# The last three steps of an expert decoding: two interleaved, the weight remainders given to another engine, 36 matmuls put behind them

## The chip, the cores and the metric

The kernel runs on one core of one Trainium2 chip. The metric is the device time of one execution in microseconds (us), the median of several runs. A core has a matrix engine (TensorE, in the profile PE, its weight loads PEld), a vector engine (VectorE, DVE), an activation engine (ScalarE, ACT), a general engine (GpSimd, POOL) and an engine that here only issues transfers (SyncE, SP). Each works through its own queue of instructions in the order in which they were written. They wait for each other through semaphores.

## The reference

One encoder layer on 512 tokens of 1024 channels in float32: a projection, a gated branch and an attention branch, an output projection, and then the part that matters here, a retrieval over 128 x 128 = 16384 small experts:

```
q = (xb @ w_query).reshape(tokens, 8 heads, 2, 128)
s = einsum('thpc,pkc->thpk', q, sub_keys)             # 2 x 128 scores per token and head
s1, i1 = top_k(s[:, :, 0], 16); s2, i2 = top_k(s[:, :, 1], 16)
cand = s1[..., :, None] + s2[..., None, :]             # 256 sums
sc, ci = top_k(cand, 16)
e = i1[ci // 16] * 128 + i2[ci % 16]                   # 16 experts per token and head
g = softmax(sc)
act = gelu(einsum('td,thkd->thk', xb, expert_u[e]))
out = einsum('thk,thkd->td', g * act, expert_v[e])
```

## The kernel before, in words

The first three blocks of 128 tokens (384 tokens) are computed densely: for each of 128 slices of 128 experts TensorE multiplies all 384 tokens with a slice of `expert_u` ("a product of U"). A fourth block goes by gathers much later.

A product of U keeps float32 precision by splitting both operands in two parts. Slice i is loaded into `uraw` by SyncE's queue (`load`, two buffers). ScalarE rounds it into `uhi` (`part`, line 171, two buffers). Another engine subtracts, `ulo = uraw - uhi` (`part_lo`, line 182, two buffers). Then TensorE does 24 matmuls (line 202) in three passes of eight: `uhi` with the high part of the tokens, `uhi` with their low part, and `ulo` with the high part. The sum lands in a `pu` buffer (two of them), which ScalarE empties with a gelu into `act` (`flush`, line 789). A load needs the `uraw` buffer of the slice two before, which is free when that slice's `ulo` is made.

While `prog["pool"]` is true, GpSimd makes `ulo` in two halves, issued from `part` and inside `product`. Once it is false, the caller `los()` has VectorE make it whole.

`ahead(n, limit)` issues the next n matmuls of U. It is the filler: it is called between steps of the routing, whose long work is on VectorE. AHEAD = 31 products are to be done by the end of the routing. The routing runs so:

- For each of 16 query slices `scores` gives `sc`, and VectorE finds the 16 best in three lists (`top16`, lines 624 to 632). `candidates` (line 648) and `pick_head` (`top16` on `cand`) follow for each head. `decode` turns the choice into expert numbers for groups of 3, 3 and 2 heads. It is a generator with five pieces: comparisons on VectorE (lines 670 to 688), nothing, copies by ScalarE into one-hot tiles `oh` (lines 697 and 698, first from `rw`, then from `cl`), products on VectorE (lines 702 to 707), sums on VectorE into `route` (lines 711 to 717). `oh` has three buffers and one decoding uses two.
- `softmax` makes the gates (a subtraction on VectorE, an exponential on ScalarE, a normalisation on VectorE).
- At the end of the 16 slices, the second decoding (heads 3 to 5) is half done, the choice for head 7 and the third decoding (heads 6 and 7) are still to come. Before the change the second one is finished, then head 7 is chosen, then the third one runs, with `ahead(24)` or `ahead(36)` between the pieces.
- `turn` transposes the three routing tables on TensorE (`idxT` and `gT`). Then a loop over 48 groups of 8 tokens follows ("the one-hot loop"): VectorE makes `ohb` (a comparison) and `oha` (its product with the gates `gw`), TensorE multiplies them in 16 small matmuls, ScalarE copies the result to `wst`, and `left // 48` or so matmuls of U fill each group. In it VectorE makes `ulo`.

After the loop the U products go on, now together with the products of `expert_v` (line 1090).

Of the kernel before, what the change touches and what calls it, by code (L numbers as in the profile page):

```python
# [11 lines left out]
BF16 = mybir.dt.bfloat16  # L12
# [3 lines left out]
ALU = mybir.AluOpType  # L16
# [11 lines left out]
NK = 128  # L28
# [10 lines left out]
AHEAD = 31  # L39
# [7 lines left out]
def peer_block(ctx: ExitStack, tc: tile.TileContext, A, out):  # L47
    nc = tc.nc
    V, S, G, T, Q = nc.vector, nc.scalar, nc.gpsimd, nc.tensor, nc.sync
# [89 lines left out]
    iota_b = keep.tile([128, NK], BF16, name="iota_b")  # L139
# [18 lines left out]
    prog = {"u": 0, "gen": None, "gelu": None, "pool": True}  # L158
    halves = {}

    def load(i):
        if i < NQ + NK:
            raws[i] = upool.tile([128, KT, 128], F32, name="uraw")
            Q.dma_start(raws[i], A["w_q"][i] if i < NQ else A["uT"][i - NQ])
# [12 lines left out]
    def part_lo(i, eng=G):  # L177

        if i in halves:
            hi, lo = parts[i]  # L180
            k = slice(4 * halves[i], 4 * halves[i] + 4 if eng is G else KT)
            eng.tensor_tensor(lo[:, k, :], raws[i][:, k, :], hi[:, k, :].bitcast(F32), op=ALU.subtract)  # L182
            halves[i] += k.stop // 4 - halves[i]
            if halves[i] == 2:
                del raws[i], halves[i]

    def los():
        for i in list(halves):
            part_lo(i, V)
# [68 lines left out]
    def drain(gen, n=10 ** 6):  # L258
        for _ in range(n):
            if next(gen, True):  # L260
                return
# [22 lines left out]
    def heads_T(which, rot):  # L284


        for p in range(4):
            ps = pr.tile([128, 512], F32, name=("tr", "po")[p % 2])
            for b in range(NB):
                T.transpose(ps[:, b * 128:(b + 1) * 128], rot[:, b, p * 128:(p + 1) * 128], ident)  # L290
            two = tk.tile([128, 2, 512], F32R, name="qk2", tag="qk", bufs=8)
            klo = h2T[1][:, 2 * p:2 * p + 2, :]
            for j in range(2):
                own, other = (slice(64 * i, 64 * i + 64) for i in (j, 1 - j))
                hi = two[own, j, :]
                S.copy(hi, ps[own])
                lo = two[other, j, :] if which == "q" else klo[own, j, :]
                V.tensor_tensor(lo, ps[own], hi.bitcast(F32), op=ALU.subtract)
                if which == "k":
                    G.tensor_copy(two[other, j, :], hi.bitcast(F32))  # L300
                    G.tensor_copy(klo[other, j, :], lo.bitcast(F32))
            qk[which].append((two, klo if which == "k" else None))
            yield
# [39 lines left out]
    turning = heads_T("q", rot)  # L343
# [25 lines left out]
    turning = heads_T("k", rot)  # L369
# [25 lines left out]
    for b in range(NB):  # L395
        t = va[:, b, :]
# [168 lines left out]
    for b in range(NB):  # L565
        t = hs[b] = tk.tile([128, 1024], F32, name="xs", bufs=4)
# [45 lines left out]
    rt = rt_ctx.enter_context(tc.tile_pool(name="rt", bufs=1))  # L612
# [107 lines left out]
    def softmax(pool, top, g):  # L720

        PK = list(top.shape)
        V.tensor_tensor(g, top, top[:, :, :, 0:1].to_broadcast(PK), op=ALU.subtract)
        yield
        S.activation(g, g, AF.Exp)
        yield
        sm = pool.tile([128, 2, PK[1], PK[2]], F32, name="gsum")
        V.tensor_reduce(sm[:, 0], g, axis=AX.X, op=ALU.add)
        V.reciprocal(sm[:, 1], sm[:, 0])
        V.tensor_tensor(g, g, sm[:, 1, :, :, None].to_broadcast(PK), op=ALU.mult)  # L730
        yield
# [34 lines left out]
    steps = []  # L766

    def step():
        while steps:
            if next(steps[0], True) is None:  # L770
                return
            steps.pop(0)

    def pick_head(h):
        cand = cands.pop(h)
        top16([(top[:, h, b, :], ci[:, h, b, :], cand[:, b, :]) for b in range(DB)])
        h0 = 0
        for n in HG:
            if h == h0 + n - 1:
                steps.append(decode(rt, iota_v, dense[1][:, h0:h0 + n], ci[:, h0:h0 + n], [r[:, h0:h0 + n] for r in by_head]))  # L780
            h0 += n
# [3 lines left out]
    def flush():  # L785
        if prog["gelu"] is not None:
            e, o = prog["gelu"]
            acts[e] = ring.tile([128, DT], F32, name="act")
            S.activation(acts[e], o[:, :DT], AF.Gelu_apprx_tanh)  # L789
            prog["gelu"] = None  # L790

    def ahead(n, limit):

        while n > 0:
            if prog["gen"] is None:
                if prog["u"] >= min(limit, NK):
                    return
                i = prog["u"] + NQ
                load(i + 2)
                part(i + 1)  # L800
                prog["gen"] = product(i, DT)
            o = next(prog["gen"])
            n -= 1
            if o is not None:
                flush()
                prog["gelu"] = (prog["u"], o)
                prog["gen"] = None
                prog["u"] += 1

    for c in range(NQ + 1):  # L810
# [4 lines left out]
        if c >= 1:  # L815
# [4 lines left out]
                cands[(c - 1) // 2] = candidates(rt, dense, (c - 1) // 2)  # L820
            elif c > 1:
                pick_head((c - 1) // 2 - 1)
    while steps:
        ahead(24, AHEAD)
        flush()
        step()
    pick_head(H - 1)
    gating = softmax(rt, top, by_head[2])
    next(gating)
    step()  # L830
    for _ in range(4):
        ahead(36, AHEAD)
        flush()
        next(gating, None)
        step()
    assert not steps or next(steps[0], True)
    tsc = {}

    def turn(b):

        rows = []
        for nm, t, dt, scale in (("i2T", route[1], BF16, 1.0), ("i1T", route[0], BF16, 1.0),
                                 ("gT", route[2], F32, GSCALE)):
            ps = pr.tile([128, 512], F32, name="po" if nm == "i2T" else "tr")
            T.transpose(ps[:, :128], t[:, b].rearrange("p h k -> p (h k)"), ident)
            if nm == "i2T":

                idx = rt.tile([128, 16, 2, 8, 2], BF16, name="idxT", bufs=2)
            r = idx[:, :, len(rows), :, :] if dt is BF16 else rt.tile([128, 16, 8, 2], F32, name=nm)
            S.activation(r, ps[:, :128].rearrange("p (g t) -> p g t", t=8)[:, :, :, None].to_broadcast([128, 16, 8, 2]),  # L850
                         AF.Copy, scale=scale)
            rows.append(r)
        gT = rows[2]
        yield

        gw = rt.tile([128, 16, 8, 2, 2], F16, name="gw", bufs=2)
        V.tensor_copy(gw[:, :, :, 0], gT)
        V.tensor_tensor(gw[:, :, :, 1], gT, gw[:, :, :, 0], op=ALU.subtract)

        gs = rt.tile([128, 16, 2], F32, name="gs", bufs=2)  # L860
        V.tensor_copy(gs[:, :, 0], gw[:, :, 7, 0, 0])
        V.tensor_tensor(gs[:, :, 1], gT[:, :, 7, 0], gs[:, :, 0], op=ALU.subtract)
        tsc[b] = (idx, gw, gs)
        yield

    drain(turn(0))
    prog["pool"] = False


    half = [128, 16, NK // 2, 2]  # L870

    def hots(t8):


        b, g = divmod(t8, 16)
        idx, gw, gs = tsc[b]
        pairs = lambda t: t.rearrange("p s t two -> p (s t) two")[:, :, None, :].to_broadcast(half)
        c = rt.tile([128, 16, NK], BF16, name="ohb", bufs=3)
        a = rt.tile([128, 16, NK], F16, name="oha", tag="oh", bufs=3)
        V.tensor_tensor(c.rearrange("p s (k two) -> p s k two", two=2),  # L880
                        iota_b.rearrange("p (k two) -> p k two", two=2)[:, None, :, :].to_broadcast(half),
                        pairs(idx[:, g]), op=ALU.is_equal)
        wide = [128, 7, 2, NK // 2, 2]
        V.tensor_tensor(a[:, 0:14].rearrange("p (t s) (k two) -> p t s k two", s=2, two=2),  # L884
                        c[:, 8:15, None].rearrange("p t o (k two) -> p t o k two", two=2).to_broadcast(wide),
                        gw[:, g, 0:7, :, None, :].to_broadcast(wide), op=ALU.mult)
        rest.append((a, c, gs, g))
        return a, c
# [9 lines left out]
    N8 = DT // 8  # L898
    per = WTOK // 8
    wst = None  # L900
    hot = [hots(0), hots(1)]
    gated()
    ahead(24, AHEAD)
    los()
# [16 lines left out]
    for t8 in range(N8):  # L921
        a, c = hot.pop(0)
# [3 lines left out]
        for q in range(2):  # L926
            pw = pr.tile([128, 4, NK], F32, name="acc", bufs=4)
            for j in range(4):
                for s in range(2):
                    t = 4 * q + j  # L930
# [7 lines left out]
        if t8 % 16 == 8 and t8 // 16 + 1 < DB:  # L938
            turning = turn(t8 // 16 + 1)
# [220 lines left out]
    for e in range(NK):  # L1160
# [18 lines left out]
        n = min(int(quota), 128 - dotted)  # L1179
# [18 lines left out]
        if e == NK - 8:  # L1198
            assert issued == 128
            fg, *rest = [upool.tile([128, 1024], F32, name="fin", tag=t) for t in ("uraw", "uhi", "ulo") for _ in range(2)]  # L1200
            last = ex.tile([128, 2, 1024], F32, name="fin", tag="uv", bufs=UVB)
# [19 lines left out]
    for b in (0, 1):  # L1221
        vproduct(NK - 1, b)
        for n in range(2):
            c = slice(n * 512, (n + 1) * 512)
# [74 lines left out]
```

## Time and profile before

| what | value |
|---|---|
| median of 3 runs | 1474.46 us (1473.89 to 1474.46) |
| profiled execution | 1474.9 us, of which the span from first to last instruction is 1473.1 us |
| TensorE busy | 98% of the span |
| VectorE busy | 78% of the span |
| ScalarE, GpSimd busy | 45%, 19% |
| mean granted TensorE clock | 0.997 of full speed |

The span and the time differ by 1.8 us that lie around the instructions. A busy share is an average over stages; in the stage of the change VectorE is busy nearly all the time too.

### The profile page before, as it was taken

To read this page: it belongs to the slowest core of one execution; us is meant where nothing else is said; L and a number is where in the kernel's file an instruction comes from. 1 tells how busy PE (TensorE), PEld (TensorE's weight loads), DVE (VectorE), ACT (ScalarE), POOL (GpSimd) and SP (SyncE) were. 2 spreads that over 40 slices of the span, in tenths; PEclk is the share of its full clock that TensorE was granted. 3 is DMA by queue.
4 is the path that set the end of the run, shared out by engine and by line. 5 is a ranking of instruction groups with operands and counts; after the bars stand their busy time and mean duration, and the time that the engine had idled before them with its cause. 6 is when DMAs were issued, how large, how long until landed. Compare 5 with 4: busy or idle time off the path is not lost.

```text
span 1473.1 us, 21706 instructions
## 1 busy us (share of the span) xinstructions
PE 1449.5 (98%) x7945; PEld 1291.3 (88%) x7945; DVE 1152.5 (78%) x2434; ACT 658.0 (45%) x1186; POOL 278.3 (19%) x222
## 2 busy tenths in 40 slices
PE   8999999999999999999999999999999999999997
PEld 6878988888999999999999999999999999988785
DVE  5745554999899949779888878888888888877865
ACT  4456743344578754433333333333333333333334
POOL 0140002445400000013131222222222222221000
PEclk9999999999999999999999999999999999999999
DMA  6331032232367776579999998999999999988764
GB/s 232 113 103 36 23 130 104 74 97 92 115 248 267 275 276 215 165 264 368 351 332 336 330 341 318 335 332 345 331 336 339 327 326 338 321 299 302 232 215 152
DMA packets 129067, 358.54 MB, mean 243 GB/s; under 512 B 9152, under 2 KB 59840, under 8 KB 112576
## 3 DMA queue, kind: packets, MB, share of 16 engines
q1 hardware_dynamic: 103328, 197.49, 40.5%
q0 software_dynamic: 18432, 134.23, 23.8%
q10 hardware_dynamic: 7200, 25.44, 4.3%
q8 instruction: 62, 1.02, 0.3%
q14 instruction: 45, 0.37, 0.1%
HBM read 327.10 MB, written 30.02 MB: 242 GB/s over the span
## 4 chain that ended last, share of the span: by engine, by line
PE 82%; DVE 11%; ACT 3%; issue 2%; DMA 1%; POOL 1%; ACTq 0%; SPq 0%; POOLq 0%; DVEq 0%
PE acc L1090 34%; PE pu L202 32%; PE acc L253 8%; DVE ohb L880 3%; DVE ulo L182 2%; DVE oha L884 2%; PE pu L253 1%; PE tr L440 1%; PE acc L453 1%; PE po L453 1%; DMA vraw<-in_uv_dram 1%; POOL ulo L182 1%; ACT uhi L171 1%; DMA uraw<-in_uT_dram 1%; PE pu L419 0%
## 5 line engine op out<-in xcount | busy, mean ns | idle before, releaser
L202 PE MATMUL pu<-h2T,uhi 128*128 128x384 f32 (+2 forms) x2336 | 450.2, 342 | 1.8 <-ACT uhi L171 0.9
L202 PEld LDWEIGHTS pu<-h2T,uhi 128*128 128x128 f32 x2336 | 408.8, 188 | 18.1 <-ACT uhi L171 1.2
L1025 POOL DMA_INDIRECT uv<-in_uv_dram,ei x128 | 172.1, 1344 | 664.4 <-DVE xlast L1040 295.9
L82 DVE TENSOR_TENSOR vlo<-vraw,vhi 128x1024 fp32r<-128x1024 f32 x126 | 154.4, 1226 | 152.6 <-ACT vhi L81 152.5
L81 ACT CAST vhi<-vraw 128x1024 fp32r<-128x1024 f32 x126 | 132.5, 1052 | 304.7 <-issue 193.3
L202 PE MATMUL pu<-h2T,ulo 128*128 128x384 f32 (+2 forms) x1168 | 235.1, 340 | 2.6 <-POOL ulo L182 2.6
L1090 PE MATMUL acc<-vhi,wahi 128*128 128x512 f32 x756 | 234.9, 391 | 0.0
L1090 PE MATMUL acc<-vlo,wahi 128*128 128x512 f32 x756 | 234.6, 391 | 0.0
L1090 PE MATMUL acc<-vhi,walo 128*128 128x512 f32 x756 | 234.2, 391 | 0.0
L202 PEld LDWEIGHTS pu<-h2T,ulo 128*128 128x128 f32 x1168 | 204.2, 188 | 7.8 <-POOL ulo L182 3.4
L1090 PEld LDWEIGHTS acc<-vlo,wahi 128*128 128x128 f32 x756 | 141.5, 188 | 32.4 <-DVE vlo L82 1.4
L1090 PEld LDWEIGHTS acc<-vhi,walo 128*128 128x128 f32 x756 | 141.5, 188 | 31.0 <-DVE walo L82 0.7
L171 ACT CAST uhi<-uraw 128x1024 fp32r<-128x1024 f32 x144 | 150.4, 1045 | 40.7 <-DMA uraw<-in_uT_dram 34.6
L1040 DVE SCALAR_TENSOR_TENSOR xlast<-uv,dot,xlast 128x1024 f32<-128x1024 f32 x128 | 164.4, 1285 | 4.5
L789 ACT ACTIVATE act<-pu 128x384 f32<-128x384 f32 x128 | 62.9, 491 | 232.9 <-PE pu L202 232.8
L1090 PEld LDWEIGHTS acc<-vhi,wahi 128*128 128x128 f32 x756 | 140.6, 188 | 23.5
L1031 DVE SCALAR_TENSOR_TENSOR uv<-uv,h 128x1024 f32<-128x1024 f32 x128 | 153.8, 1219 | 7.9 <-DMA uv<-in_uv_dram,ei 7.6
L182 DVE TENSOR_TENSOR ulo<-uraw,uhi 128x1024 fp32r<-128x1024 f32 x116 | 141.5, 1219 | 18.4 <-ACT uhi L171 12.1
L182 POOL TENSOR_TENSOR ulo<-uraw,uhi 128x512 fp32r<-128x512 f32 x56 | 79.3, 1439 | 198.3 <-PE acc L253 104.8
L1068 DVE TENSOR_TENSOR wa<-act,wt 128x384 f32<-128x384 f32 x128 | 70.5, 551 | 0.8 <-DMA wt<-wd 0.8
L82 DVE TENSOR_TENSOR walo<-wa,wahi 128x384 fp32r<-128x384 f32 x126 | 69.6, 552 | 0.6 <-ACT wahi L81 0.6
L81 ACT CAST wahi<-wa 128x384 fp32r<-128x384 f32 x126 | 64.1, 509 | 9.1 <-DVE wa L1068 9.1
(274 smaller groups left out, 1511.5 us busy)
## 6 DMA issues: line engine op xcount, KB each, us to landing
uraw<-in_uT_dram SPq DMA_DIRECT2D x128, 512.0 KB, 5.9
vraw<-in_uv_dram SPq DMA_DIRECT2D x128, 512.0 KB, 5.6
wd<-wst ACTq DMA_DIRECT2D x48, 512.0 KB, 3.6
wt<-wd SPq DMA_DIRECT2D x32, 768.0 KB, 11.1
wraw<-in_w_in_dram SPq DMA_DIRECT2D x19, 512.0 KB, 3.7
uraw<-in_w_q_dram SPq DMA_DIRECT2D x16, 512.0 KB, 3.9
xT<-in_xT_dram SPq DMA_DIRECT2D x8, 256.0 KB, 3.6
xt<-in_x_dram SPq DMA_DIRECT2D x1, 2048.0 KB, 11.1
```

What stands on the lines that cost most here:

```text
L81: S.copy(hi, src)
L82: sub.tensor_tensor(lo, src, hi.bitcast(F32), op=ALU.subtract)
L171: S.copy(hi, raws[i])
L182: eng.tensor_tensor(lo[:, k, :], raws[i][:, k, :], hi[:, k, :].bitcast(F32), op=ALU.subtract)
L202: T.matmul(o, l[:, k, :], r[:, k, t0:n], start=(p == 0 and k == 0), stop=(p == 2 and k == KT - 1))
L253: T.matmul(out[b], l[:, b * 128:(b + 1) * 128], r[:, kk, :], start=(k == 0 and i == 0), stop=(k == KT - 1 and i == 2))
L789: S.activation(acts[e], o[:, :DT], AF.Gelu_apprx_tanh)
L1025: G.indirect_dma_start(out=uvs[r].rearrange("p s d -> p (s d)"), out_offset=None, in_=A["uv"], in_offset=bass.IndirectOffsetOnAxis(ap=ei[: ...
L1031: V.scalar_tensor_tensor(uv[:, 0, :], uv[:, 0, :], 1.0, h2, op0=ALU.mult, op1=ALU.mult, accum_out=d[:, 0:1])
L1040: V.scalar_tensor_tensor(xlast, uv[:, 1, :], d[:, 1:2], xlast, op0=ALU.mult, op1=ALU.add)
L1068: eng.tensor_tensor(wa.rearrange("p (c t) -> p c t", c=NWC), acts.pop(e).rearrange("p (c t) -> p c t", c=NWC), wts[e // WG][:, :, e % WG, ...
L1090: T.matmul(acc[b][n], l[:, c], r[:, n * 512:(n + 1) * 512], start=(e == 0 and i == 0), stop=(e == NK - 1 and i == 2))
```

## The change

GpSimd's part in `ulo` ends when the 16 slices are done, not after the first `turn`. From there `chunk(n)` issues n matmuls of U, then VectorE's `ulo` for each slice that has been split, then the gelu. The two last decodings are interleaved: head 7 is chosen ahead of the products of the second decoding, and the comparisons of the third come before the sums of the second. Until the transposes 216 matmuls of U are issued where there were 252 (with the 12 that both have before); the 36 that are missing go to the one-hot loop, which has 504 matmuls of U to place where it had 468. The first comparison `ohb` is written ahead of the four small operations that split the gates.

```diff
-    while steps:
-        ahead(24, AHEAD)
+
+    prog["pool"] = False
+
+    def chunk(n):
+        ahead(n, AHEAD)
+        los()
         flush()
-        step()
+
+    chunk(24)
+    step()
     pick_head(H - 1)
+    last = steps.pop()
     gating = softmax(rt, top, by_head[2])
     next(gating)
+    chunk(24)
     step()
-    for _ in range(4):
-        ahead(36, AHEAD)
-        flush()
-        next(gating, None)
-        step()
-    assert not steps or next(steps[0], True)
+    next(last)
+    chunk(24)
+    step()
+    step()
+    next(gating)
+    next(last)
+    next(last)
+    chunk(36)
+    next(gating)
+    next(last)
+    chunk(36)
+    next(last)
+    chunk(36)
+    chunk(24)
+    assert not steps and next(last, True) and next(gating, True)
...
-        yield
+        yield idx
...
-    drain(turn(0))
-    prog["pool"] = False
...
+    def match(ix):
+        c = rt.tile([128, 16, NK], BF16, name="ohb", bufs=3)
+        V.tensor_tensor(... op=ALU.is_equal)
+        return c
...
-    hot = [hots(0), hots(1)]
+    turning = turn(0)
+    first = match(next(turning)[:, 0])
+    drain(turning, 1)
+    hot = [hots(0, first), hots(1)]
```

VectorE's queue after the last list of the 16 slices, before the change: from the last candidates straight to the products of the second decoding (`oh`), then its sums, and no `ulo` in sight.

```order
L632 MAX_INDEX i_2180<-s_2179,sc 128x8 x3
L648 TENSOR_TENSOR cand<-s_2179 128x3x16
L648 TENSOR_TENSOR cand<-s_2179 128x3x8
L648 TENSOR_TENSOR cand<-s_2179 128x3x10
L648 TENSOR_TENSOR cand<-s_2179 128x3x12
L648 TENSOR_TENSOR cand<-s_2179 128x3x8
L702 TENSOR_TENSOR oh<-oh,iota_v 128x1728 x2
L705 TENSOR_TENSOR oh<-oh,fi 128x9x64
```

The same place of VectorE's queue in the changed kernel.

```order
L648 TENSOR_TENSOR cand<-s_2179 128x3x8
L182 TENSOR_TENSOR ulo<-uraw,uhi 128x1024
L624 MAX top<-cand 128x8 x3
L626 MAX_INDEX ci<-top,cand 128x8 x3
L628 MATCH_REPLACE cand<-top,cand 128x54 x3
L630 MAX top<-cand 128x8 x3
L632 MAX_INDEX ci<-top,cand 128x8 x3
L723 TENSOR_TENSOR route_2188<-top 128x8x3x16
L182 TENSOR_TENSOR ulo<-uraw,uhi 128x1024
L702 TENSOR_TENSOR oh<-oh,iota_v 128x1728 x2
```

The `ulo` of the third slice of U (product 2, counted from 0) now stands behind all the list work of the routing, and the next one behind the choice for head 7. Six more follow before the first `ohb`: one ahead of the sums of the second decoding, one behind them, and the rest around the end of the third.

ScalarE's queue in the changed kernel, from the exponential of the softmax on (`rw` and `cl` are here those of the third decoding).

```order
L789 ACTIVATE act<-pu 128x384
L725 ACT_TABLE_LOAD
L725 ACTIVATE route_2188<-route_2188 128x8x3x16
L697 CAST oh<-rw 128x6x128
L698 CAST oh<-rw 128x6x64
L697 CAST oh<-cl 128x6x128
L698 CAST oh<-cl 128x6x64
L171 CAST uhi<-uraw 128x1024
L789 ACT_TABLE_LOAD
L789 ACTIVATE act<-pu 128x384 x2
```

Before, two `uhi` and a gelu stood between the exponential and these four copies. Now the copies come first, and the next `uhi` and the next two gelus stand behind them.

TensorE's queue at the transposes of the routing tables, before and in the changed kernel as one piece of the difference (`uhi` and `ulo` rows are products of U).

```order
 L202 MATMUL pu<-h2T_110,ulo 128x384 x8
-L202 MATMUL pu<-h2T_110,uhi 128x384 x8
-L202 MATMUL pu<-h2T_111,uhi 128x384 x8
-L202 MATMUL pu<-h2T_110,ulo 128x384 x8
-L202 MATMUL pu<-h2T_110,uhi 128x384 x8
+L862 MATMUL po<-ident,route_2187 128x128
+L862 MATMUL tr<-ident,route_2186 128x128
+L862 MATMUL tr<-ident,route_2188 128x128
```

The transposes move up by 36 matmuls; until there TensorE's queue reads the same in both kernels.

## Rows read from the trace of the kernel before

**Rows 1.** The page, part 1: busy time and share of the span of each engine.

```profile
PE 1449.5 (98%) x7945; PEld 1291.3 (88%) x7945; DVE 1152.5 (78%) x2434; ACT 658.0 (45%) x1186; POOL 278.3 (19%) x222
```

**Rows 2.** Two stretches, one just after a long wait of TensorE and one in the one-hot loop. Columns: us, busy time (with instructions) of PE, PEld, DVE, ACT and POOL, granted TensorE clock, DMA share, GB/s.

```profile
368.25:371.60 3.35, 3.31 (x11) 2.80 (x10) 3.32 (x10) 0.97 (x2) 3.35 (x3) 0.50 0.42 155
...
395.40:526.90 131.50, 129.06 (x1226) 120.37 (x1225) 129.17 (x122) 104.38 (x234) 0.00 (x0) 1.00 0.67 248
```

**Rows 3.** TensorE in order of time, from the third slice of U to the transposes: start, duration, line, out<-in, shape, count, and in brackets the idle time before it with what ended it.

```profile
348.69 2.93 PE L202 MATMUL pu<-h2T,uhi 128*128 128x384 f32 x16
351.46 1.55 PE L202 MATMUL pu<-h2T,ulo 128*128 128x384 f32 x8
353.75 3.06 PE L202 MATMUL pu<-h2T,uhi 128*128 128x384 f32 x16 [0.74 <-ACT act L789]
...
367.69 2.89 PE L202 MATMUL pu<-h2T,ulo 128*128 128x384 f32 x8 [2.56 <-POOL ulo L182]
...
375.15 2.93 PE L202 MATMUL pu<-h2T,uhi 128*128 128x384 f32 x16
...
379.31 2.93 PE L202 MATMUL pu<-h2T,uhi 128*128 128x384 f32 x16
...
389.72 0.27 PE L845 MATMUL po<-ident,route 128*128 128x128 f32 x1
```

**Rows 4.** VectorE in order of time: the comparisons of the first decoding (its first and the next row after it), and then from the comparisons of the second decoding to its products.

```profile
299.14 0.22 DVE L670 CAST cf<-ci 128x144 f16<-128x144 uint32 x1
...
302.62 0.59 DVE L648 TENSOR_TENSOR cand<-s 128x48 f32<-128x48 f32 x5
...
343.46 0.47 DVE L670 CAST cf<-ci 128x144 f16<-128x144 uint32 x1
...
345.88 2.56 DVE L680 TENSOR_TENSOR at<-at,mk 128x144 f16<-128x144 f16 x2
...
349.77 0.67 DVE L624 MAX8 s<-sc 128x8 f32<-128x128 f32 x3
...
353.29 0.43 DVE L624 MAX8 top<-cand 128x8 f32<-128x54 f32 x3
...
355.64 0.67 DVE L624 MAX8 s<-sc 128x8 f32<-128x128 f32 x3
...
359.15 0.58 DVE L648 TENSOR_TENSOR cand<-s 128x48 f32<-128x48 f32 x5
359.65 2.02 DVE L702 TENSOR_TENSOR oh<-oh,iota_v 128x1728 bf16<-128x1728 bf16 x2
```

**Rows 5.** VectorE in order of time, the sums of the second decoding, the choice for head 7, and the first and last row of the comparisons of the third decoding with the row after it.

```profile
363.66 0.82 DVE L711 TENSOR_TENSOR oh<-oh 128x576 bf16<-128x576 bf16 x2
...
365.77 0.73 DVE L717 TENSOR_TENSOR route<-oh 128x144 f32<-128x144 bf16 x2
366.41 0.45 DVE L624 MAX8 top<-cand 128x8 f32<-128x54 f32 x3
...
369.23 1.30 DVE L670 CAST cf<-ci 128x96 f16<-128x96 uint32 x1
...
376.67 0.54 DVE L728 TENSOR_REDUCE gsum<-route 128x24 f32<-128x384 f32 x1
```

**Rows 6.** VectorE's group for `ulo` on the page: count, busy time, mean ns of one, idle time before.

```profile
L182 DVE TENSOR_TENSOR ulo<-uraw,uhi 128x1024 fp32r<-128x1024 f32 x116 | 141.5, 1219 | 18.4 <-ACT uhi L171 12.1
```

**Rows 7.** ScalarE in order of time: a load of a function table, and the copies of the third decoding from `cl` with the split and the gelu behind them.

```profile
371.12 1.28 ACT L725 ACT_TABLE_LOAD   x1
...
379.27 0.83 ACT L697 CAST oh<-cl 128x768 bf16<-128x768 int32 x1
...
380.42 1.05 ACT L171 CAST uhi<-uraw 128x1024 fp32r<-128x1024 f32 x1
381.37 0.48 ACT L789 ACTIVATE act<-pu 128x384 f32<-128x384 f32 x1
```

**Rows 8.** The loads of slices of U that SyncE's queue issued from 345 to 395 us: count, size, median us from issue to landing.

```profile
uraw<-in_uT_dram SPq DMA_DIRECT2D x11, 512.0 KB, 3.6
```

**Rows 9.** TensorE in order of time in the one-hot loop and behind it. L931 rows are the 16 small matmuls that begin a group of 8 tokens.

```profile
395.37 1.05 PE L931 MATMUL acc<-oha,ohb 128*128 128x128 f16 x16
...
418.45 1.07 PE L931 MATMUL acc<-oha,ohb 128*128 128x128 f16 x16
...
422.34 1.06 PE L931 MATMUL acc<-oha,ohb 128*128 128x128 f16 x16
...
472.40 1.07 PE L931 MATMUL acc<-oha,ohb 128*128 128x128 f16 x16
...
475.11 1.07 PE L931 MATMUL acc<-oha,ohb 128*128 128x128 f16 x16
475.98 1.99 PE L202 MATMUL pu<-h2T,uhi 128*128 128x384 f32 x10
...
527.82 3.02 PE L202 MATMUL pu<-h2T,uhi 128*128 128x384 f32 x16
...
533.10 3.05 PE L202 MATMUL pu<-h2T,uhi 128*128 128x384 f32 x16 [0.87 <-ACT uhi L171]
```

**Rows 10.** The stretch from VectorE's first `ohb` to its last `oha`: first VectorE's busy time (then clock, DMA share, GB/s), and then PE, PEld, DVE and POOL on `ulo` alone.

```profile
393.00:526.90 133.90, 131.53 (x125) 1.00 0.67 247
...
393.00:526.90 133.90, 34.58 (x162) 27.32 (x160) 24.35 (x20) 0.00 (x0) 1.00 0.67 247
```

More of the change, by code (lines that the diff above doesn't have):

```diff
@@ L864, in turn, with hots @@
         yield
-    drain(turn(0))
-    prog["pool"] = False
     half = [128, 16, NK // 2, 2]
-    def hots(t8):
+    def match(ix):
+        c = rt.tile([128, 16, NK], BF16, name="ohb", bufs=3)
+        V.tensor_tensor(c.rearrange("p s (k two) -> p s k two", two=2),
+                        iota_b.rearrange("p (k two) -> p k two", two=2)[:, None, :, :].to_broadcast(half),
+                        ix.rearrange("p s t two -> p (s t) two")[:, :, None, :].to_broadcast(half), op=ALU.is_equal)
+        return c
+    def hots(t8, c=None):
         b, g = divmod(t8, 16)
         idx, gw, gs = tsc[b]
-        pairs = lambda t: t.rearrange("p s t two -> p (s t) two")[:, :, None, :].to_broadcast(half)
-        c = rt.tile([128, 16, NK], BF16, name="ohb", bufs=3)
+        c = match(idx[:, g]) if c is None else c
         a = rt.tile([128, 16, NK], F16, name="oha", tag="oh", bufs=3)
-        V.tensor_tensor(c.rearrange("p s (k two) -> p s k two", two=2),
-                        iota_b.rearrange("p (k two) -> p k two", two=2)[:, None, :, :].to_broadcast(half),
-                        pairs(idx[:, g]), op=ALU.is_equal)
         wide = [128, 7, 2, NK // 2, 2]
```

## Prediction

> **What bounds the kernel now.** I read the page first: TensorE is busy for 98% of the span [rows 1]. So a change can only win by filling TensorE's waits, and it loses by every new one. The second view is TensorE in order of time at the place of the change [rows 3]. The reader is to see that it runs there almost without a gap, on products of U, although VectorE is far behind. Only two waits stand out, 0.74 us on a gelu and 2.56 us on GpSimd's `ulo`. The third view is the granted clock: after the 2.56 us wait it is 0.50, the 1.2 GHz level, for 3.35 us [rows 2]. The fourth is VectorE at the same time [rows 4, 5]. It works without a break on lists that TensorE delivered long before. At 351.46, when TensorE begins the third pass of product 2 [rows 3], VectorE is still sorting the lists of slice 14, and it reaches the products of the second decoding at 359.65. So VectorE trails by some 8 us, and that costs nothing as long as no product of U needs VectorE.
>
> **First wait.** The change puts the `ulo` of product 2 into VectorE's queue behind all that list work. When does VectorE get there? It starts the comparisons of the second decoding at 343.46. In this execution they take 5.80 us (the next sort begins at 349.77, with candidates of 0.50 ahead of it); 2.56 us of it is one pair of additions, which ran while GpSimd had an `ulo` to make [rows 4]. The first decoding's comparisons, alone, took 302.62 - 299.14 = 3.48 us. GpSimd is now quiet, so I take 3.48. Then candidates 0.50 (359.15 to 359.65), a sort 3.52 (349.77 to 353.29), a choice 2.35 (to 355.64), a sort 3.51 (to 359.15), candidates 0.50: VectorE is at the new `ulo` at 343.46 + 13.86 = 357.32, and ends it 1.22 us later [rows 6], at 358.5. TensorE needs it at 351.46: **a wait of 7.1 us** (9.4 if the comparisons stay at 5.80).
>
> **Second wait.** Choice for head 7 and subtraction 2.82 (366.41 to 369.23) [rows 5], the next `ulo` 1.22, products of the second decoding 4.01 (359.65 to 363.66) [rows 4, 5], comparisons of the third decoding, `ulo` 1.22. These comparisons were 7.44 us (369.23 to 376.67) beside GpSimd; the wider tile took 3.48 alone; I take 3.3, since the work is narrower and GpSimd is silent, with 7.4 as the upper bound. 358.5 + 2.8 + 1.2 + 4.0 + 3.3 + 1.2 = 371.1. TensorE meanwhile ends the third pass (1.4), does product 3 (4.16, from 375.15 to 379.31 [rows 3]) and two passes of product 4 (2.8), so it stands at 366.9 and **waits 4.2 us**. The slices of U are no tighter bound: a load is issued when VectorE has made the `ulo` two slices before, at 358.5, lands 3.6 later [rows 8] and is split by 363.2, before product 4 begins at 364.1. GpSimd's queue has nothing behind its `ulo` that anyone waits for in this stage.
>
> **Third wait.** ScalarE's queue now holds the four copies of the third decoding ahead of the next split and the gelu that frees the `pu` buffer of product 5. The copy from `cl` needs an `oh` buffer, and the first free one is given back by the second decoding's first sum, which VectorE does behind the `ulo` above: 371.1 + 2.1 (363.66 to 365.77) + 0.4 (half of the 0.73 pair) = 373.6 [rows 5]. Then copies 1.15 (379.27 to 380.42), split 0.95 (to 381.37), table load 1.28, gelu 0.48 [rows 7]: 377.5. TensorE ended product 4 at 372.5: **a wait of 5.0 us**. Behind it I find no further wait: products 5 to 8 take 4 x 4.16, and the transposes come at 394.1. Before they came at 389.72 [rows 3], so this stage ends 4.4 us later, with 36 matmuls fewer done.
>
> **The clock.** The one long wait in the rows was followed by 3.35 us at 0.50, which is some 1.7 us of work lost [rows 2]. After the first and second wait such a loss falls into the next wait (4.2 and 5.0 us). After the third it counts. Bounds 0 and 1.7; I take 1.3, nearer to the only row. The Trainium skill, "TensorE: Matmul & The Clock Gate", section "HAM oscillation", says that a stream of matmuls with gaps falls back to the low clock at each and restarts cold; this speaks against a change that makes three gaps. By that rule the term is the row's full 1.7 and the sum 0.4 more; the trace's one long gap agrees with it.
>
> **The one-hot loop.** From the transposes to the first group took 5.65 us (to 395.37 [rows 3, 9]); 24 matmuls of U fill it in both kernels, so I keep it. The comparison ahead of the gate split is counted at nothing: those 24 matmuls (4.16 us) cover it, and without that cover it would be worth about one comparison, 1.2 us. The loop ran from 395.37 to 527.82, 132.45 us. An undisturbed group takes 2.71 (472.40 to 475.11) with 10 matmuls of U in 1.84 (behind 0.87 of small ones), 0.184 each; 10.5 of them make 2.80, times 48 is 134.4. The two later transposes cost 3.89 - 2.71 = 1.18 each [rows 9]. VectorE must do 133.9 us with 20 `ulo` now [rows 10], 135.1 with 21, so TensorE's 136.8 is the bound. Of the 132.45 now, 47 x 2.71 + 2 x 1.18 + 0.87 = 130.6 are work, so about 1.9 go to waits; with VectorE's slack of 1.7 most of them should go, and I add 0.7 (bounds 0 and 1.9). 137.5 - 132.45 = 5.05: the 36 matmuls, 6.2 us at full rate, are taken in for a little less. Their last 10 stand behind the last group and hide the 0.87 us at 533.10 [rows 9].
>
> **Sum.** 4.4 + 1.3 + 5.05 - 0.87 = 9.9 us. The profiled execution took 1474.9, so it would be 1484.8; that execution is 0.4 above the median of the runs, and against the median, 1474.46, I forecast **1484.4**. Later stages are TensorE's and shift as a whole.
>
> **Rivals.** About 0.2%, 2.9 us, is what a measurement of this kernel can tell from no change.
> - *Only two waits.* If the `oh` buffer is free earlier, or ScalarE does the gelu in time, product 5 starts at 372.5; about 1 us of wait on the `ulo` of product 6 follows, and the transposes come at 390.2. Sum 0.5 + 1.3 + 5.05 - 0.87 = 6.0: **1480.4**. For it speaks that the buffer's turn is read from code and not from a row.
> - *VectorE is as slow without GpSimd as with it.* Then 2.3 and 4.1 us come on top, half of it perhaps: +3.2, **1488**. The clean 3.48 us speaks against it.
> - *The waits in front are as before.* Then the transposes come 36 matmuls, 6.2 us, earlier, and the sum is -6.2 + 5.05 - 0.87 = -2.0: **1472.4**, no change that can be told. It needs VectorE at the first moved `ulo` by 351.5.
> - *Faster.* VectorE, freed of GpSimd, does its list work so much faster that no product waits; then the 0.74, the 2.56 and the 1.7 at low clock are won too: -7.0, **1467.4**. It decides when the 9.4 us of sorts and choices between 349.77 and 359.15 take under 3.5. No GpSimd stretch is seen in them: two sorts there take 3.52 and 3.51, alike.
>
> **How the numbers follow.** Three waits 0.62, two 0.15, the slow VectorE 0.10, as before 0.08, faster 0.05. The first alone has its range from 1481 to 1487 (clock 0 to 1.7, waits in the loop 0 to 1.9, comparisons a little longer). To leave out no more than 2 in 10, it must reach down to the second and up to the third: **1478 to 1489**. Faster 0.05, same 0.08, slower 0.87.
>
> **What would show it.** TensorE's waits on `ulo` by VectorE of some 7 and 4 us and on `act` of some 5 us before the transposes, which come near 394 to 396; a granted clock of 0.50 after them; one-hot groups of 2.7 to 2.9 us with hardly a wait on `oha`; and no wait on `uhi` just behind the loop. The forecast is wrong if VectorE reaches the first moved `ulo` by 352, or if the loop stays at 132 us in spite of its 36 matmuls.

## The result, and the profile after

The changed kernel takes 1485.06 us (median of 6 runs, 1484.45 to 1486.19), the kernel before 1474.46 us beside it. The ratio is 1.007, with a 95% interval of 1.0059 to 1.0081: slower by 0.7%. The forecast was 1484.4 us, in a range of 1478 to 1489.

The profiled execution has a span of 1483.4 us, against 1473.1 before. The page of it, part 1 (answers to [rows 1]):

```profile
PE 1450.6 (98%) x7945; PEld 1294.5 (87%) x7945; DVE 1153.4 (78%) x2444; ACT 657.7 (44%) x1186; POOL 246.1 (17%) x202
```

Nothing of the loss is seen here. TensorE's share is 98% as before. Its busy time is 1.1 us higher for the same 7945 instructions, of which more ran at the low clock (below). Only GpSimd's share has moved, 19% to 17%. The loss has to be looked for in the stage. TensorE in order of time (answers to [rows 3]):

```profile
349.03 2.94 PE L202 MATMUL pu<-h2T,uhi 128*128 128x384 f32 x16
359.20 2.93 PE L202 MATMUL pu<-h2T,ulo 128*128 128x384 f32 x8 [7.24 <-DVE ulo L182]
361.93 3.03 PE L202 MATMUL pu<-h2T,uhi 128*128 128x384 f32 x16
...
371.41 2.19 PE L202 MATMUL pu<-h2T,ulo 128*128 128x384 f32 x8 [2.29 <-DVE ulo L182]
377.88 5.19 PE L202 MATMUL pu<-h2T,uhi 128*128 128x384 f32 x16 [4.27 <-ACT act L789]
382.90 1.56 PE L202 MATMUL pu<-h2T,ulo 128*128 128x384 f32 x8
...
396.79 0.27 PE L862 MATMUL po<-ident,route 128*128 128x128 f32 x1
```

Three waits stand where the forecast had them: on the first low part by VectorE, on its third, and on the gelu that empties a `pu` buffer. (All times of this execution are 0.34 us later than before's already when TensorE enters the stage.) VectorE (answers to [rows 4, 5]) shows what the first two wait for, and ScalarE (answers to [rows 7]) the third:

```profile
343.79 0.48 DVE L670 CAST cf<-ci 128x144 f16<-128x144 uint32 x1
...
346.23 0.50 DVE L680 TENSOR_TENSOR at<-at,mk 128x144 f16<-128x144 f16 x2
...
347.55 0.60 DVE L648 TENSOR_TENSOR cand<-s 128x48 f32<-128x48 f32 x5
...
357.93 1.22 DVE L182 TENSOR_TENSOR ulo<-uraw,uhi 128x1024 fp32r<-128x1024 f32 x1
...
361.88 1.22 DVE L182 TENSOR_TENSOR ulo<-uraw,uhi 128x1024 fp32r<-128x1024 f32 x1
...
370.14 1.22 DVE L182 TENSOR_TENSOR ulo<-uraw,uhi 128x1024 fp32r<-128x1024 f32 x1
```

```profile
373.83 0.83 ACT L697 CAST oh<-cl 128x768 bf16<-128x768 int32 x1 [2.62 <-DVE route L717]
374.57 0.51 ACT L698 CAST oh<-cl 128x384 bf16<-128x384 int32 x1
374.98 1.04 ACT L171 CAST uhi<-uraw 128x1024 fp32r<-128x1024 f32 x1
376.04 1.28 ACT L789 ACT_TABLE_LOAD   x1
377.33 0.87 ACT L789 ACTIVATE act<-pu 128x384 f32<-128x384 f32 x2
```

The comparisons of the second decoding take 3.76 us (343.79 to 347.55), with GpSimd quiet from 344.19 on, where they took 5.80. VectorE has no break from there to 374.1, and reaches the first low part at 357.93, 6.0 us after TensorE began to wait for it (359.20 - 7.24 = 351.96). ScalarE's copy from `cl` waits 2.62 us for VectorE's sums, and the split, the table load and the gelu stand behind it.

Three stretches of the changed kernel, the two at the low clock and the one-hot loop (columns as in [rows 2]):

```profile
355.27:362.10 6.83, 2.90 (x9) 2.90 (x10) 6.83 (x48) 0.00 (x0) 0.00 (x0) 0.50 0.22 77
372.34:382.58 10.24, 5.97 (x20) 5.46 (x19) 8.24 (x17) 5.28 (x7) 0.00 (x0) 0.50 0.31 102
402.44:539.70 137.26, 135.40 (x1280) 127.58 (x1279) 130.59 (x123) 108.21 (x239) 0.00 (x0) 1.00 0.68 253
```

TensorE was at 0.50, the 1.2 GHz level, twice, for 6.83 and 10.24 us. It worked for 2.90 and 5.97 us of that, so 1.45 and some 3.0 us of work were lost. The loop ran at full clock and took 137.26 us.

So the time went here: the first transpose comes at 396.79 instead of 389.72 (+7.07, with the 0.34), the loop takes 137.26 instead of 132.45 (+4.81), and from the loop's end to the first matmul with `expert_v` it is 25.25 instead of 26.19 us (-0.94). Together +10.9; the stages behind, which the change does not touch, were 0.6 us shorter in this execution.

### The profile page after: what moved, and what is told of

It reads as the page before. It is cut to its first block, busy times and chain, and to the rows that moved or that the text cites. A ratio compares the mean times of both kernels' runs of the same rounds, so it can differ in the third digit from the quotient of the medians.

```text
span 1483.4 us, 21692 instructions
## 1 busy us (share of the span) xinstructions
PE 1450.6 (98%) x7945; PEld 1294.5 (87%) x7945; DVE 1153.4 (78%) x2444; ACT 657.7 (44%) x1186; POOL 246.1 (17%) x202
## 4 chain that ended last, share of the span: by engine, by line
PE 90%; DVE 7%; ACT 1%; DMA 1%; issue 0%; SPq 0%; ACTq 0%; DVEq 0%
PE pu L202 38%; PE acc L1110 34%; PE acc L253 8%; PE acc L951 3%; PE pu L253 1%; PE tr L440 1%; PE acc L453 1%; PE po L453 1%; DMA vraw<-in_uv_dram 1%; DVE i L632 1%; DVE sc L628 1%; DVE i L626 0%; PE pu L419 0%; PE pu L418 0%; PE tr L755 0%
## 5 line engine op out<-in xcount | busy, mean ns | idle before, releaser
L182 DVE TENSOR_TENSOR ulo<-uraw,uhi 128x1024 fp32r<-128x1024 f32 x126 | 153.8, 1221 | 32.2 <-ACT uhi L171 32.1
L182 POOL TENSOR_TENSOR ulo<-uraw,uhi 128x512 fp32r<-128x512 f32 x36 | 46.7, 1319 | 182.4 <-ACT uhi L171 182.4
```

## The experiments

The theory: VectorE trails TensorE by some 8 us at the end of the 16 slices. That costs nothing while no product of U needs VectorE in time, and the change lets the lateness reach TensorE, through VectorE's queue and through ScalarE's. The rivals: the low parts by VectorE are the loss in themselves; or the new order is; or the 36 matmuls are. Ratios are to the kernel before, whose median beside these runs was 1474.4 to 1475.0 us. The table puts the executions side by side, each interval worked out from two rows of its trace: A from the first matmul of U behind the scores (the rows `tr<-keys,qT`) to the first transpose, B from there to the first group of the one-hot loop, C from that group to the first matmul with `expert_v`, D to the end.

| kernel | median us | A | B | C | D |
|---|---|---|---|---|---|
| before | 1474.46 | 47.4 | 5.65 | 158.6 | 919.1 |
| changed | 1485.06 | 54.1 | 5.65 | 162.5 | 918.5 |
| changed, low parts by GpSimd | 1483.74 | 52.8 | 5.65 | 162.4 | 918.6 |
| before, low parts by VectorE | 1480.71 | 53.4 | 6.6 | 158.4 | 918.4 |
| before, 36 matmuls moved | 1476.47 | 44.6 | 6.6 | 162.5 | 919.1 |
| changed, copies later | 1478.96 | 47.9 | 5.65 | 162.4 | 919.4 |
| changed, switch one product later | 1487.03 | 54.6 | 5.65 | 162.5 | 921.3 |
| changed, shorter lists | 1483.36 | 52.8 | 5.65 | 162.4 | 918.3 |
| before, comparison ahead | 1474.20 | 47.6 | 5.4 | 158.6 | 919.9 |
| before, comparison ahead, 12 moved | 1474.46 | 46.3 | 7.0 | 158.2 | 918.5 |
| third order, 12 moved | 1469.52 | 42.0 | 5.4 | 158.9 | 919.4 |
| third order, 24 moved | 1472.92 | 42.0 | 5.4 | 160.1 | 922.1 |

**The changed kernel with the low parts left to GpSimd.**

```diff
-    prog["pool"] = False
     def chunk(n):
         ahead(n, AHEAD)
-        los()
+        if not prog["pool"]:
+            los()
         flush()
...
     drain(turning, 1)
+    prog["pool"] = False
```

> The changed kernel, but GpSimd goes on making the low parts of U until the first one-hot groups, as in the kernel before. Theory (VectorE trails by some 8 us, and the new order lets that lateness reach TensorE through every queue): the two waits on ulo by VectorE vanish, but ScalarE's copies of the third decoding still stand ahead of the gelu that frees product 5's buffer, and they wait for VectorE's first L717 sum, so TensorE, which is at product 5 by 361, waits there in one piece for 12 to 18 us: 1481 to 1487 us. Rival (the low parts by VectorE are the loss themselves): no wait over 3 us, 36 matmuls moved, 1472 to 1474 us.

1483.74 us, ratio 1.0063 (1.0050 to 1.0076). All waits on `ulo` are gone, and one wait of 14.4 us has taken their place. TensorE's row, and two stretches of that kernel, within the wait and behind it:

```profile
375.50 5.49 PE L202 MATMUL pu<-h2T,uhi 128*128 128x384 f32 x16 [14.41 <-ACT act L789]
```

```profile
365.60:375.50 9.90, 0.00 (x0) 0.00 (x0) 9.69 (x36) 5.26 (x8) 1.77 (x1) 0.50 0.00 0
375.50:382.40 6.90, 6.89 (x25) 6.90 (x26) 6.83 (x12) 2.32 (x3) 4.37 (x4) 0.59 0.43 146
```

It is the third wait of the changed kernel, now in one piece: VectorE was busy for 9.69 of the 9.90 us shown, and ScalarE's copies, which waited for it (6.30 us for `rw`, 1.47 for the sums), held the gelu. So the low parts by VectorE are not the loss in themselves. With or without them the order makes TensorE wait for VectorE.

**The kernel before with the low parts given to VectorE.**

```diff
+    prog["pool"] = False
     while steps:
         ahead(24, AHEAD)
+        los()
         flush()
...
         ahead(36, AHEAD)
+        los()
         flush()
```

> The kernel before, with its order, but VectorE makes the low parts of U from the end of the list loop on. Theory: the first wait is that of the changed kernel, 7 us on VectorE's ulo of product 2, and 0 to 4 us of smaller waits follow, with 0 to 2 us at the low clock; the one-hot loop stays at 132 us: 1482 to 1488 us. Rival (the new order makes the waits, by ScalarE's queue): below 1476 us.

1480.71 us, ratio 1.0036 (1.0024 to 1.0049), a little under the theory's 1482. The first wait is there in the old order too, and the routes come late:

```profile
359.13 2.93 PE L202 MATMUL pu<-h2T,ulo 128*128 128x384 f32 x8 [7.22 <-DVE ulo L182]
...
396.04 0.42 PE L848 MATMUL po<-ident,route 128*128 128x128 f32 x1 [1.83 <-DVE route L717]
```

So the order with its moved matmuls alone costs 8.9 us, the low parts alone 5.8 (both against 1474.89 beside them), and the two together not 14.7 but 10.6. They do not add up; by the theory both pay for the same lateness of VectorE.

**The kernel before with only the 36 matmuls moved.**

```diff
-    for _ in range(4):
-        ahead(36, AHEAD)
+    for r in range(4):
+        if r < 3:
+            ahead(36, AHEAD)
```

> The kernel before, with only the last 36 matmuls of U ahead of the transposes left to the one-hot loop. Theory (the loop takes them in for a little less than they cost ahead of it, 4.8 for 6.2 us, and the wait of 0.9 us behind the loop is hidden): transposes 6.2 us earlier, 1472 to 1474 us. Rival (the routes are not ready earlier, or the loop is bound by VectorE beside them): 1474.5 us or more, with a wait at the transposes.

1476.47 us, ratio 1.0012 (1.0003 to 1.0020). The rival holds: 6.2 us of matmuls less bring the transposes only 2.6 us forward, since the routes are not there.

```profile
387.10 0.44 PE L846 MATMUL po<-ident,route 128*128 128x128 f32 x1 [4.28 <-DVE route L717]
```

A falls by 2.8 and C grows by 3.9; 0.9 more is lost in B, where the granted clock was 0.50 from 387.19 to 390.60. Behind this kernel's wait on GpSimd, 2.55 us as in the kernel before and ending at 367.74, the clock did not fall (next to last column):

```profile
367.70:371.20 3.50, 3.18 (x17) 2.86 (x18) 3.46 (x15) 1.19 (x2) 3.50 (x3) 1.00 0.36 109
```

**ScalarE's copies 24 matmuls later.**

```diff
     next(last)
-    next(last)
-    chunk(36)
+    chunk(24)
+    next(last)
+    chunk(12)
```

> The changed kernel, with ScalarE's four copies of the third decoding issued 24 matmuls later, behind the next split and the gelu that frees product 5's buffer. Theory: the first two waits stay (7.2 and 2.3 us), the third (4.3 us on act) and the low clock behind it (2.3 us) go, and a wait of about 1 us on the ulo of product 6 comes: 1479 to 1481 us. Rival (VectorE's lateness is due there anyway, and the time goes to the next ulo): 1484 to 1486 us.

1478.96 us, 6.1 less than the changed kernel, and A is 6.3 shorter. TensorE's waits from 300 to 575 us (us in total, times, longest):

```profile
PE pu L202 <- DVE ulo L182: 9.2, 3, 7.2
PE tr L863 <- ACT idxT L868: 2.2, 3, 0.9
PE pu L202 <- ACT uhi L171: 0.6, 1, 0.6
```

The wait of 4.3 us on `act` is gone. On `ulo` the first wait stands (7.23), the second is 1.33 us, and one of 0.65 is new. The second stretch at the low clock is gone, but the first lasts longer than in the changed kernel:

```profile
352.82:363.06 10.24, 4.94 (x15) 4.95 (x16) 10.24 (x59) 0.41 (x1) 0.00 (x0) 0.50 0.18 56
```

So the third wait came from the place of the copies in ScalarE's queue: VectorE's sums come no earlier (ScalarE's copy from `cl` still waits 2.63 us for them), but the gelu that frees the `pu` buffer no longer stands behind them.

**GpSimd keeps the first moved low part.**

```diff
     chunk(24)
+    prog["pool"] = False
     step()
     pick_head(H - 1)
```

(`prog["pool"] = False` ahead of `chunk` is left out, and `chunk` calls `los()` only behind the switch.)

> The changed kernel, but GpSimd still makes the low part of the first moved product, and VectorE those from the next product on. Theory (VectorE is late as a whole, and any product that needs it first pays): the wait of 7.2 us moves to the next product and shrinks by the one ulo that VectorE is spared, to 6.0 to 6.5 us; the later waits stay: 1483 to 1485 us. Rival (the place of that one ulo in VectorE's queue is the cause): the 7.2 us vanish, 1477 to 1479 us.

1487.03 us, ratio 1.0083 (1.0069 to 1.0097). The rival falls: the wait of 7.03 us stands one product later. But it has not shrunk, and the theory's number was missed on that. VectorE's row and TensorE's:

```profile
345.89 2.60 DVE L680 TENSOR_TENSOR at<-at,mk 128x144 f16<-128x144 f16 x2
```

```profile
363.90 2.93 PE L202 MATMUL pu<-h2T,ulo 128*128 128x384 f32 x8 [7.03 <-DVE ulo L182]
```

While GpSimd made that low part (from 345.86, 2.54 us), VectorE's pair of additions took 2.60 us, as before [rows 4]. In the changed kernel the same pair took 0.50. So VectorE was spared 1.2 us and paid 2.1. D was 921.3 in this execution, nearly 3 us longer than in the changed kernel; of that, 1.1 us are waits of TensorE on `wahi`, an operand of the products of `expert_v` (near 1371 and 1376), and what the rest is stays open. By A to C this kernel is 0.5 us slower than the changed one.

**The lists of four slices made shorter.** This kernel leaves out a part of the sorting, so it computes something else.

```diff
-        for m, ix, s in lists:
-            V.match_replace(s, m[:, 0:8], s, NEG)
+        if not short:
+            for m, ix, s in lists:
+                V.match_replace(s, m[:, 0:8], s, NEG)
```

> The changed kernel, with the three MATCH_REPLACE of each of the sorts of slices 12 to 15 left out, so these lists hold their first eight entries twice: VectorE has 4 x 0.78 = 3.1 us less to do ahead of the end of the decoding, in a stretch in which it never waits, and nothing else changes. Theory (the first wait is VectorE's lateness, one for one): 7.2 falls to 4.1 us, the later waits stay: 1481 to 1482.5 us. Rival (the waits are set by ScalarE's queue or by the loads of U, whose buffers come free late): 1484 to 1486 us.

1483.36 us: 8.3 above the kernel before beside it, where the changed kernel is 10.6 above its own. That is less of a gain than the theory's 1481 to 1482.5. The first wait fell from 7.24 to 5.39 us, not to 4.1:

```profile
356.60 2.93 PE L202 MATMUL pu<-h2T,ulo 128*128 128x384 f32 x8 [5.39 <-DVE ulo L182]
```

```profile
341.48 0.78 DVE L671 CAST cf<-ci 128x144 f16<-128x144 uint32 x1
342.30 1.18 DVE L672 TENSOR_SCALAR mk<-cf 128x144 f16<-128x144 f16 x1
343.40 0.18 DVE L675 TENSOR_SCALAR mk<-cf 128x144 f16<-128x144 f16 x1
```

VectorE came to the comparisons early enough to fall beside a low part of GpSimd's (340.90, 2.52 us). The first two operations took 0.78 and 1.18 us there, 1.3 more than in the changed kernel, where they took 0.48 and 0.20. So 3.1 - 1.3 = 1.8 us of earliness came through, and 1.85 us of the wait went. The lateness counts one for one at the first wait, and the rival falls. The second wait is 1.80 us and the third, on `act`, 4.80, and behind the third the low clock went on to 381.05:

```profile
374.22:381.05 6.83, 5.79 (x18) 5.79 (x19) 5.72 (x11) 2.56 (x5) 0.00 (x0) 0.50 0.27 81
```

**The first comparison alone ahead of the gate split**, in the order of before.

```diff
-    drain(turn(0))
-    prog["pool"] = False
...
+    turning = turn(0)
+    first = match(next(turning)[:, 0])
+    drain(turning, 1)
+    prog["pool"] = False
+    hot = [hots(0, first), hots(1)]
```

> The kernel before, with only the first one-hot comparison taken ahead of the gate split. Theory (24 matmuls of U cover it): no change, 1474 to 1475.5 us. Rival (the first group waits for VectorE, so a comparison of 1.2 us is won): 1473.3 us.

1474.20 us, ratio 0.9993 (0.9984 to 1.0002): no change that can be told. In the profiled execution B is 0.3 us shorter.

**The same with 12 matmuls moved.**

```diff
-        ahead(36, AHEAD)
+        ahead(36 if r < 3 else 24, AHEAD)
```

> The kernel before, with the comparison ahead of the gate split and the last 12, not 36, matmuls of U left to the one-hot loop. Theory (12 matmuls ahead of the transposes, 2.07 us, are about what the routes are early by, as the run with 36 moved showed, and the loop takes 12 in for some 1.6 us; the wait of 0.87 us behind the loop may go): no wait for a route at the transposes and 1472.8 to 1474.5 us. Rival (the routes are not ready even then): a wait of 1 to 2 us there, 1475 to 1476 us.

1474.46 us, ratio 0.9997 (0.9988 to 1.0006). The time is the theory's, the rows are the rival's: a wait of 1.79 us for the routes, and a low clock behind it (B is 7.0). It is no loss in this execution, where the loop takes the 12 in for nothing (C is 0.4 shorter than before).

**A third order.** If the lateness is the cause, VectorE may take the low parts over once it has caught up. Before, GpSimd kept TensorE waiting at product 5 (367.69 in [rows 3]), and VectorE ended the products of the second decoding at 363.66 [rows 5], 1.3 us before TensorE could begin the third pass (364.97). That is where this kernel switches. GpSimd's lateness there goes with VectorE's work, too. A row of the chain of work that led to this wait in the kernel before (start, us, what):

```profile
360.68 6.97 POOL ulo L182
```

Half a low part took GpSimd 6.97 us here, where the median of its halves in this stage is 1.30, and VectorE did the products and sums of the second decoding meanwhile (359.65 to 366.50). That VectorE held it up is read from these times; no run tests it alone. Each low part is put ahead of routing work that is not due yet, and ScalarE's copies behind the gelu. `chunk` is that of the first experiment, and the first comparison stands ahead of the gate split.

```diff
-    while steps:
-        ahead(24, AHEAD)
-        flush()
-        step()
+    chunk(24)
+    step()
+    chunk(24)
+    step()
+    chunk(24)
+    prog["pool"] = False
+    chunk(24)
+    step()
+    chunk(24)
     pick_head(H - 1)
     gating = softmax(rt, top, by_head[2])
     next(gating)
+    chunk(24)
     step()
-    for _ in range(4):
-        ahead(36, AHEAD)
-        flush()
-        next(gating, None)
-        step()
+    next(gating)
+    chunk(24)
+    step()
+    step()
+    next(gating)
+    step()
+    chunk(24)
+    step()
+    chunk(36)
```

> A third order of the end: VectorE makes the low parts only from the product on which GpSimd kept TensorE waiting before, at a place where VectorE has caught up (between the second decoding's products and its sums), each low part stands ahead of work that is not due yet, ScalarE's copies of the third decoding stand behind the gelu, 12 matmuls are moved, and the first comparison stands ahead of the gate split. Theory (a low part by VectorE costs TensorE nothing where VectorE comes to it before the third pass): the waits of 2.6 us on POOL and of 7, 2 and 4 us of the changed kernel are all gone or under 1.5 us, and so is the low clock: 1468 to 1471 us. Rival (VectorE has no room for the low parts anywhere ahead of the transposes): the routes come later, a wait of 4 us or more at the transposes, 1474 us or more.

1469.52 us, ratio 0.9965 (0.9951 to 0.9979): 4.9 us faster than the kernel before beside it, and 15.5 less than the changed kernel. TensorE and VectorE, where the 2.56 us stood, and TensorE at the transposes:

```profile
364.95 1.61 PE L202 MATMUL pu<-h2T,ulo 128*128 128x384 f32 x8
...
384.39 0.33 PE L862 MATMUL po<-ident,route 128*128 128x128 f32 x1 [0.34 <-DVE route L717]
```

```profile
363.62 1.23 DVE L182 TENSOR_TENSOR ulo<-uraw,uhi 128x1024 fp32r<-128x1024 f32 x1
...
372.63 0.20 DVE L670 CAST cf<-ci 128x96 f16<-128x96 uint32 x1
...
375.74 1.22 DVE L182 TENSOR_TENSOR ulo<-uraw,uhi 128x1024 fp32r<-128x1024 f32 x1
```

VectorE ended the low part at 364.85, TensorE began the third pass at 364.95 without a wait. The comparisons of the third decoding take VectorE 3.11 us (372.63 to 375.74), where they took 7.44 beside GpSimd [rows 5]. The stage in one row, of the kernel before and of this one:

```profile
341.50:390.00 48.50, 45.16 (x252) 43.83 (x250) 45.88 (x194) 24.85 (x33) 32.68 (x21) 0.96 0.35 117
```

```profile
341.50:384.40 42.90, 41.38 (x239) 40.26 (x237) 42.55 (x198) 23.86 (x32) 10.05 (x8) 1.00 0.36 122
```

The granted clock is 1.00 all through. VectorE makes six low parts, 7.3 us of new work, and is still busy 3.3 us less, with GpSimd beside it for 10 us instead of 33. A is 5.4 us shorter. Of that 2.1 are the 12 matmuls, which C takes in for 0.3. The rest, some 3.3 us, is the wait of 2.56 us with the 1.7 lost at the low clock behind it, less two small new waits (0.53 on `act`, 0.34 at the transposes). With the 12 moved and the comparison ahead, but in the order of before, nothing was won (the run above). No run has this order with all low parts left to GpSimd, so the switch and the order are not told apart, except by the rows.

**The third order with 24 moved.**

```diff
-    chunk(36)
+    chunk(24)
```

> The same with 24 matmuls moved instead of 12. Theory (VectorE's routes, not TensorE, set when the transposes come, so matmuls moved beyond that leave a wait): a wait of 2 to 3.5 us at the transposes and 0.5 to 2 us more time than with 12 moved. Rival (the loop takes more matmuls in for less): as fast or faster than with 12 moved.

1472.92 us, ratio 0.9991 (0.9982 to 1.0000). The transposes come no earlier behind the scores (A is 42.0 in both), with a wait of 2.33 us:

```profile
383.96 0.33 PE L862 MATMUL po<-ident,route 128*128 128x128 f32 x1 [2.33 <-DVE route L717]
```

By the medians it is 3.4 us slower than with 12, more than the theory's 0.5 to 2. By A to C it is 1.2 us slower. D is 2.6 us longer in the profiled execution, and 2.3 us of that are waits on `wahi` (near 1372 and 1378), which the run with 12 hasn't. Why they come is open.

## Why the prediction was right, step by step

- **First wait: 7.1 us forecast, 7.24 measured.** The sum over VectorE's queue put it at the low part at 357.32; it was there at 357.93 - 0.34 = 357.6. The choice that decided it, comparisons of 3.48 us and not 5.80, was near: 3.76. Sorts and choices took as long as before.
- **Second wait: 4.2 forecast, 2.29 measured.** VectorE's part was right (the low part done at 371.1; measured 371.36 - 0.34 = 371.0). The difference is TensorE's: after the first wait 1.45 us went at the low clock, as the prediction's step on the clock had said of this place, and some 0.4 are small differences of both engines. This miss costs nothing, since the third wait ends with the gelu, which comes by VectorE and ScalarE: at 377.88 - 0.34 = 377.54, forecast 377.5.
- **Third wait: 5.0 forecast, 4.27 measured.** The turn of the `oh` buffers, read from the code, is in the row: the copy from `cl` waits for `route` of L717 and starts at 373.83 - 0.34 = 373.5, forecast 373.6. TensorE came 0.8 us later than forecast, most of it through the low clock of its last pass (2.19 instead of 1.55 us).
- **The clock: 1.3 forecast, between 0 and 1.7; this term was mis-sized.** Product 5's first two passes took 5.02 us (377.88 to 382.90) instead of 2.77, so the loss behind the third wait was 2.25. The upper bound came from a single row, 3.35 us after a wait of 2.56. Here the low clock began at 372.34, before the third wait, and went on for 4.70 us behind it (377.88 to 382.58). How much of the low clock falls behind a wait is not in the one row: it was 2.90 us behind the first wait here, 4.94 behind the same wait with the copies later, and 5.79 behind the third wait with the shorter lists, where the low clock began only within that wait (374.22). So a wait shortly before is not needed for a loss this large. The Trainium skill, "TensorE: Matmul & The Clock Gate", section "HAM oscillation", where matmuls fall to the low clock at each gap and start cold behind it, spoke for the full 1.7 of the row, which was nearer. The long waits here agree with the fall, but not with one loss for each. Of the short ones, 2.55 us with 36 matmuls moved and 2.33 with 24 moved in the third order left the granted clock at 1.00.
- **Transposes: 395.4 forecast (394.1 and the clock), 396.79 - 0.34 = 396.45 measured.** Of the 1.0 us, 0.95 is the clock's.
- **The one-hot loop: 137.5 forecast, 137.26 measured.** Groups take 2.71 us with 10 matmuls of U (478.25 to 480.96) and 2.88 with 11 (to 483.84), and beside the transposes one wait is left in it, 0.59 us at 404.10, where 0.7 was added for waits. The five other kernels with 36 matmuls moved have 162.4 to 162.5 in the table's C, whatever the order of the stage ahead. Behind the loop 0.94 us were won, forecast 0.87.
- **The comparison ahead of the gate split: nothing forecast, and no change in the medians where it was changed alone**; in that profiled execution B is 0.3 us shorter.

The sum was +9.9 and the medians differ by 10.6. The rivals *only two waits*, *VectorE as slow as beside GpSimd*, *waits as before* and *faster* did not come: there are three waits, the comparisons ran calm, and sorts and choices took as long as before. Three of them rest on something true all the same. *Only two waits* is what the kernel with the copies later shows, with its A 0.5 us above that of before, as that rival had it. Beside GpSimd VectorE is slower, by 2.1 us where one low part stays there, but in the changed kernel nothing is left for it to run beside. And in *waits as before* (1472.4 us) the step that has the transposes come 6.2 us earlier fails in the order of before: with the 36 matmuls moved the routes were only 2.6 us early, and the time was 1476.47. For *faster* the prediction says that no GpSimd stretch is seen in the sorts; GpSimd did work beside most of the second of them (353.39, 5.04 us), and that sort took 3.51 us as the first took 3.52, so there was nothing to win.

## What to carry to other kernels

A filler that keeps the bottleneck engine busy works only as long as it needs nothing from the engine whose lateness it covers. Before giving such filler work to a trailing engine, compare, for each piece, the time at which the engine's in-order queue comes to it with the time at which it is due, and look also at third engines whose queue carries both the trailing engine's results and the filler's. Here giving the low parts to VectorE cost 5.8 us by itself where VectorE trailed, and was part of an order 4.9 us faster than before where it had caught up.

## What the runs showed of the hardware

- **GpSimd's subtraction and some operations of VectorE hold each other up; the sorts are not held.** A pair of additions in 16 bit took 2.60 us beside it and 0.50 without; a cast and a scalar operation 0.78 and 1.18 instead of 0.48 and 0.20. A choice for a head took 2.35 us beside it (from 353.29 in the kernel before) and 2.35 without (from 351.58 in the changed one). The other way round, half a low part took GpSimd 6.97 us beside VectorE's products and sums, where the median is 1.30. The Trainium skill, "GPSIMD Engine Reference", section "Key points", says that GpSimd shares its SBUF interfaces with VectorE and contends with VectorE's instructions in a two-port mode or with two inputs in SBUF; the additions, which have two inputs, agree, and in which mode the cast and the scalar operation ran, no run here shows. So a low part costs VectorE 1.22 us if it makes it, and cost it 2.1 where GpSimd made it beside the additions.
- **The low clock lasts for unequal times.** Behind a wait of 2.56 us in the kernel before it was at 0.50 for 3.41 us, and behind one of 2.55 with 36 matmuls moved not at all. Waits of 7.24 and 7.23 us came with 6.83 us of it (the changed kernel) and 10.24 (copies later). The wait's length alone does not tell it.
